# The last norm of a two-layer encoder: 1/rms by ScalarE's root and a Newton step on VectorE, and the last quarter's squares and sum in one VectorE instruction

## The chip, the cores and the metric

The kernel runs on one core of one Trainium2 chip. A core has five engines that each work through a queue of their own, in order: TensorE (PE in the profile; PEld is its loading of weights), VectorE (DVE), ScalarE (ACT), GpSimd (POOL) and SyncE (SP, which here only starts transfers). They wait for one another by semaphores. The metric is the time of one execution on the device, in microseconds; lower is better. The profile is that of one execution; it has a span (first to last instruction) that is a little shorter than the time.

## The reference

Two layers over 512 frames of 1024 channels: a half-step SwiGLU feed-forward block, a mixing block of two head groups, cross-attention into 256 memory tokens, and a second half-step feed-forward block. Behind the last layer stands a norm. All is float32.

```python
def rmsnorm(x, g):
    xf = x.astype(jnp.float32)
    y = xf * lax.rsqrt(jnp.mean(xf * xf, axis=-1, keepdims=True) + EPS)
    return (y * g.astype(jnp.float32)).astype(x.dtype)

def swiglu(h, w1, w3, w2):
    return (jax.nn.silu(h @ w1) * (h @ w3)) @ w2

def reference(...):
    for l in range(DEPTH):
        x = x + 0.5 * swiglu(rmsnorm(x, ffn1_norm[l]), ffn1_w1[l], ffn1_w3[l], ffn1_w2[l])
        ...
        x = x + 0.5 * swiglu(rmsnorm(x, ffn2_norm[l]), ffn2_w1[l], ffn2_w3[l], ffn2_w2[l])
    return rmsnorm(x, final_norm)
```

The change is in the last line: the norm of the result, frame by frame, and what stands around it at the end of the program.

## The kernel before

Through nearly all of the program the activations lie transposed, channels on the 128 partitions and the 512 frames in the columns. Weights come in by transfers from SyncE (some are added to others on the way by transfers that GpSimd starts, line 134); ScalarE and VectorE split each weight into a rounded high part and the rest (lines 76 and 77), and a product is three matmuls (`mm3`, lines 84 to 86).

The last block is `finish`. There the second product of the last feed-forward block is computed with frames on the partitions, so that a frame's norm is a sum along a row. There are four blocks of 128 frames; `y[i]` holds block i, 128 x 1024. `turn(i)` first brings the residual into `y[i]` (transposes on TensorE, copies on ScalarE, line 1127). Blocks 0 and 1 are accumulated together, weight by weight, in four PSUM tiles of 512 columns. Then TensorE makes block 2 in two halves, then the first half of block 3 (`k` in the code), then its second half in two quarters of 256 columns, and ends.

For each piece `add` adds half of the PSUM tile to `y` on VectorE (line 1132), and ScalarE squares the result with a sum along the row into a column of `ss` (line 1134, fss in the profile; an ACTIVATE and the reading of the accumulator). `sums` adds two such columns and makes v = sum/1024 + 1e-6 on VectorE (lines 1138 and 1139, fv). `scale` then takes v to the power -1/2 on GpSimd (line 1146, fcol), multiplies both halves of `y` by that column and by the gain on VectorE (lines 1150 and 1152), and sends them out, the first half from ScalarE's queue (line 1151) and the second from SyncE's (line 1153).

Block 3 is the one that ends the program. Its first half is multiplied by the gain ahead of time (line 1180), so that ScalarE can scale it by the column alone (`ahead`, line 1148) while VectorE does the second half. Its v is made from the first three quarters ahead of time, and the last quarter's sum is added by line 1188.

What order these instructions have on each engine is decided by the framework's scheduler when the program is built, from the order of the code and a model of times; the engines then keep to it. At the program's end, line 1297, SyncE waits for all outputs to land, each engine drains (it waits until what it has started is done) and reports to GpSimd by a semaphore, and GpSimd lets all of them go; this happens twice.

Of the kernel before, what the change touches and what calls it, by code (L numbers as in the profile page):

```python
# [7 lines left out]
F32 = mybir.dt.float32  # L8
F32R = mybir.dt.float32r
I32 = mybir.dt.int32  # L10
AF = mybir.ActivationFunctionType
ALU = mybir.AluOpType
AX = mybir.AxisListType

P = 128
D = 1024
# [30 lines left out]
def trunk_kernel(ctx: ExitStack, tc: tile.TileContext, ap: dict, out: bass.AP):  # L47
    nc = tc.nc
    pe, act, dve, pool = nc.tensor, nc.scalar, nc.vector, nc.gpsimd
# [3 lines left out]
    tp = ctx.enter_context(tc.tile_pool(name="tp", bufs=2))  # L53
    sm = ctx.enter_context(tc.tile_pool(name="sm", bufs=3))
# [3 lines left out]
    def acc_tile():  # L58
        return pacc.tile([P, 512], F32, tag="acc", name="acc")

    def ps_tile():
        return pp.tile([P, 512], F32, tag="ps", name="ps")
# [5 lines left out]
    def s_tile(shape, dt, name):  # L68
        return sp.tile(shape, dt, tag="s", name=name)
# [12 lines left out]
    def mm3(o, a, b, start, stop, more=False):  # L82

        pe.matmul(o, a[0], b[0], start=start, stop=False, skip_group_check=more)  # L84
        pe.matmul(o, a[0], b[1], start=False, stop=False, skip_group_check=more)  # L85
        pe.matmul(o, a[1], b[0], start=False, stop=stop, skip_group_check=more)  # L86
# [205 lines left out]
    nhalf = const.tile([P, 4], F32, name="nhalf")  # L292
# [822 lines left out]
    def finish(a):  # L1115
        n = len(a)
        gain = s_tile([P, D], F32, "gain")
        nc.scalar.dma_start(gain, ap["final_norm"].broadcast_to([P, D]))
        y = [s_tile([P, D], F32, "y") for _ in range(NT)]
        ss = sm.tile([P, NT, 3], F32, tag="fss", name="fss", bufs=1)  # L1120

        def turn(i):
            for hf in range(2):
                ps = ps_tile()
                for c in range(4):
                    pe.transpose(ps[:, c * P:(c + 1) * P], xT[hf * 4 + c][:, i * P:(i + 1) * P], ident)
                act.copy(y[i][:, hf * 512:(hf + 1) * 512], ps)

        def add(i, at, ps, lo, hi):

            yi = y[i][:, lo:hi]
            dve.scalar_tensor_tensor(yi, ps, 0.5, yi, op0=ALU.mult, op1=ALU.add)
            sq = tp.tile([P, 512], F32, tag="sq", name="fsq", bufs=4)
            act.activation(sq[:, :hi - lo], yi, AF.Square, accum_out=ss[:, i, at:at + 1])

        def sums(i):
            v = sm.tile([P, 1], F32, tag="fv", name="fv", bufs=4)
            dve.tensor_tensor(v, ss[:, i, 0:1], ss[:, i, 1:2], op=ALU.add)
            dve.tensor_scalar(v, v, 1.0 / D, EPS, op0=ALU.mult, op1=ALU.add)
            return v  # L1140

        def scale(i, v, ahead=False):

            y0, y1, sl = y[i][:, :512], y[i][:, 512:], slice(i * P, (i + 1) * P)
            col = sm.tile([P, 1], F32, tag="fcol", name="fcol", bufs=4)
            pool.tensor_tensor(col, v, nhalf[:, 0:1], op=ALU.pow)
            if ahead:
                act.activation(y0, y0, AF.Copy, scale=col)
            else:
                dve.scalar_tensor_tensor(y0, y0, col, gain[:, :512], op0=ALU.mult, op1=ALU.mult)  # L1150
            nc.scalar.dma_start(out[0, sl, :512], y0)
            dve.scalar_tensor_tensor(y1, y1, col, gain[:, 512:], op0=ALU.mult, op1=ALU.mult)
            nc.sync.dma_start(out[0, sl, 512:], y1)

        w = {}

        def products(ps, i, js, lo, hi):
            sl = slice(i * P, (i + 1) * P)
            for j in js:
                mm3(ps, (a[j][0][:, sl], a[j][1][:, sl]), (w[j][0][:, 0, lo:hi], w[j][1][:, 0, lo:hi]), start=j == 0, stop=j == n - 1)  # L1160


        accs = {(i, hf): acc_tile() for i in range(2) for hf in range(2)}
        for j in range(n):
            w[j] = wts.next()
            for i, hf in accs:
                products(accs[i, hf], i, [j], hf * 512, (hf + 1) * 512)
                if j == n - 1:
                    add(i, hf, accs[i, hf], hf * 512, (hf + 1) * 512)
            if j < NT:  # L1170
                turn(j)
        i, k, js = 2, 3, range(n)
        accs = {(x, hf): ps_tile() for x in (i, k) for hf in range(2)}
        for hf in range(2):
            products(accs[i, hf], i, js, hf * 512, (hf + 1) * 512)
            add(i, hf, accs[i, hf], hf * 512, (hf + 1) * 512)
            scale(hf, sums(hf))
        products(accs[k, 0], k, js, 0, 512)
        add(k, 0, accs[k, 0], 0, 512)
        dve.tensor_tensor(y[k][:, :512], y[k][:, :512], gain[:, :512], op=ALU.mult)  # L1180
        scale(i, sums(i))
        for q in range(2):
            lo, ps = 512 + 256 * q, (accs[k, 1] if q else acc_tile())[:, :256]
            products(ps, k, js, lo, lo + 256)
            add(k, 1 + q, ps, lo, lo + 256)
            if q == 0:
                v = sums(k)
        dve.tensor_scalar(v, ss[:, k, 2:3], 1.0 / D, v, op0=ALU.mult, op1=ALU.add)
        scale(k, v, ahead=True)


    idle = ps_tile()
# [38 lines left out]
    for l in range(L):  # L1231
        nxt = Norm("mix_norm", l)
        if l == 0:
            ffn(norm, PLAIN[0], nxt.add, start=begin, between=early())
        else:
            ffn(norm, PLAIN[2], nxt.add)
        norm, nxt = nxt, Norm("xa_norm", l, row=False)
        mn = []
        mem = memory(l, mn)
        mix(l, norm, mem, nxt.add)  # L1240
        for _ in mem:
            pass
        norm, nxt = nxt, Norm("ffn2_norm", l)
        xattn(l, norm, mn, nxt.add)
        norm = nxt
        if l + 1 < L:
            nxt = Norm("ffn1_norm", l + 1)
            ffn(norm, PLAIN[1], nxt.add)
            norm = nxt
        else:  # L1250
            finish(ffn(norm, PLAIN[3], None))
# [49 lines left out]
```

## Time and profile before

| | us |
|---|---|
| time, median of 3 runs (lowest, highest) | 2092.37 (2092.34, 2093.55) |
| time of the profiled execution | 2092.47 |
| its span | 2090.7 |
| busy in it: PE, DVE, ACT, POOL | 2077.4, 1408.4, 918.0, 230.3 |
| TensorE's mean granted clock | 0.999 of full speed |

In the profile's rows a line stands for the instructions of one line of the kernel on one engine: the tile it writes, an arrow, what it reads, partitions x columns, and how many there are. In a timeline the first number is the start and the second the duration, both in us; in brackets stands how long the engine had been idle, and behind an arrow what ended that. An engine's name with a q is its queue: drains, semaphores and the starting of transfers, which aren't counted as busy.

### The profile page before, as it was taken

What the parts mean: (1) busy time and instruction counts of PE and PEld (TensorE: products, weight loads), DVE (VectorE), ACT (ScalarE), POOL (GpSimd) and SP (SyncE); (2) the same over time, 40 slices, a digit from 0 to 9 for tenths busy, and PEclk for the clock granted to TensorE, in tenths of its full rate; (3) what the DMA queues carried; (4) which work ended last, traced back from release to release, by engine and by line L of the source; (5) the groups of instructions that cost most, each with busy time, mean ns of one, the idle gap of its engine ahead of it and who ended that gap; (6) DMA issues with size and microseconds to landing.
All of it is one profiled execution on the core that took longest, in us unless ns stands there. A gap on an engine that the chain in (4) does not pass through costs nothing.

```text
span 2090.7 us, 29622 instructions
## 1 busy us (share of the span) xinstructions
PE 2077.4 (99%) x11538; PEld 1798.0 (86%) x11538; DVE 1408.4 (67%) x2126; ACT 918.0 (44%) x1461; POOL 230.3 (11%) x240
## 2 busy tenths in 40 slices
PE   9999999999999999999999999999999999999998
PEld 8889898888888888989888898988788888889897
DVE  7758576687655575766776685758766547668574
ACT  6425345434444343434544353445345434435253
POOL 1100000331000020000020000003410001100000
PEclk9999999999999999999999999999999999999999
DMA  5364554233432246636415646532343331574541
GB/s 188 115 186 121 147 157 156 67 101 108 140 121 87 61 131 186 156 118 176 131 61 158 190 111 184 156 104 71 102 117 130 101 116 41 152 203 129 140 143 71
DMA packets 109533, 268.35 MB, mean 128 GB/s; under 512 B 11536, under 2 KB 14608, under 8 KB 109392
## 3 DMA queue, kind: packets, MB, share of 16 engines
q1 hardware_dynamic: 93952, 224.49, 32.8%
q0 software_dynamic: 13104, 39.07, 10.6%
q10 hardware_dynamic: 2336, 2.89, 0.5%
q8 instruction: 91, 1.49, 0.3%
q14 instruction: 50, 0.41, 0.1%
HBM read 256.70 MB, written 2.10 MB: 124 GB/s over the span
## 4 chain that ended last, share of the span: by engine, by line
PE 97%; DVE 2%; issue 1%; POOL 0%; ACT 0%; POOLq 0%; DVEq 0%; ACTq 0%
PE ps L86 19%; PE ps L84 19%; PE ps L85 18%; PE acc L554 8%; PE acc L84 8%; PE acc L85 8%; PE acc L86 8%; PE acc L555 4%; PE ps L1030 1%; PE ps L1031 1%; PE ps L796 1%; DVE wlo L77 0%; PE ps L979 0%; PE ps L1096 0%; PE acc L346 0%
## 5 line engine op out<-in xcount | busy, mean ns | idle before, releaser
L77 DVE TENSOR_TENSOR wlo<-raw,whi 128x1024 fp32r<-128x1024 f32 (+1 forms) x334 | 394.5, 1202 | 72.0 <-ACT whi L76 63.7
L76 ACT CAST whi<-raw 128x1024 fp32r<-128x1024 f32 (+1 forms) x334 | 330.2, 1017 | 118.1 <-DMA raw<-in_ffn_w_dram 47.6
L85 PE MATMUL ps<-h,whi 128*128 128x512 f32 x848 | 330.0, 389 | 0.0
L84 PE MATMUL ps<-h,whi 128*128 128x512 f32 x848 | 329.9, 391 | 0.0
L86 PE MATMUL ps<-h,wlo 128*128 128x512 f32 x848 | 329.7, 390 | 0.0
L554 PE MATMUL acc<-bhl,whi 128*128 128x512 f32 x744 | 266.3, 398 | 0.0
L86 PE MATMUL ps<-bhl,wlo 128*128 128x256 f32 x744 | 210.8, 284 | 0.2
L85 PE MATMUL ps<-bhl,whi 128*128 128x256 f32 x744 | 209.9, 283 | 0.0
L84 PE MATMUL ps<-bhl,whi 128*128 128x256 f32 x744 | 209.8, 283 | 0.0
L555 PE MATMUL acc<-bhl,wlo 128*128 128x256 f32 x744 | 204.8, 281 | 0.0
L76 ACT CAST whi<-wsum 128x1024 fp32r<-128x1024 f32 x124 | 130.2, 1050 | 151.3 <-DVE wsum L165 83.9
L86 PEld LDWEIGHTS ps<-h,wlo 128*128 128x128 f32 x848 | 159.2, 188 | 33.5
L85 PEld LDWEIGHTS ps<-h,whi 128*128 128x128 f32 x848 | 159.2, 188 | 33.0
L84 PEld LDWEIGHTS ps<-h,whi 128*128 128x128 f32 x848 | 159.1, 188 | 32.9
L77 DVE TENSOR_TENSOR wlo<-wsum,whi 128x1024 fp32r<-128x1024 f32 x124 | 151.5, 1222 | 49.6 <-ACT whi L76 47.3
L554 PEld LDWEIGHTS acc<-bhl,whi 128*128 128x128 f32 x744 | 137.7, 189 | 24.0
L84 PEld LDWEIGHTS ps<-bhl,whi 128*128 128x128 f32 x744 | 141.5, 190 | 4.1
L86 PEld LDWEIGHTS ps<-bhl,wlo 128*128 128x128 f32 x744 | 141.4, 190 | 2.5 <-DVE wlo L77 1.6
L555 PEld LDWEIGHTS acc<-bhl,wlo 128*128 128x128 f32 x744 | 141.0, 190 | 2.8
L85 PEld LDWEIGHTS ps<-bhl,whi 128*128 128x128 f32 x744 | 141.6, 190 | 1.9
L134 POOL DMA_DIRECT2D wsum<-in_ffn_w_dram x62 | 53.8, 867 | 765.0 <-DMA wsum<-in_ffn_w_dram 369.6
L84 PE MATMUL acc<-ahl,whi 128*128 128x512 f32 x328 | 128.0, 390 | 0.0
(272 smaller groups left out, 4127.5 us busy)
## 6 DMA issues: line engine op xcount, KB each, us to landing
raw<-in_ffn_w_dram SPq DMA_DIRECT2D x198, 512.0 KB
wsum<-in_ffn_w_dram SPq DMA_DIRECT2D x124, 256.0 KB
wsum<-in_ffn_w_dram POOLq DMA_DIRECT2D x62, 512.0 KB, 6.7
raw<-in_w_in_dram SPq DMA_DIRECT2D x32, 512.0 KB
raw<-in_ffn_w_dram SPq DMA_DIRECT2D x62, 256.0 KB
raw<-in_w_out_dram SPq DMA_DIRECT2D x16, 512.0 KB
raw<-in_xa_wk_dram SPq DMA_DIRECT2D x16, 512.0 KB
raw<-in_xa_wq_dram SPq DMA_DIRECT2D x16, 512.0 KB
```

Source lines behind the costliest of these rows:

```text
L76: act.copy(hi, src)
L77: dve.tensor_tensor(lo, src, hi.bitcast(F32), op=ALU.subtract)
L84: pe.matmul(o, a[0], b[0], start=start, stop=False, skip_group_check=more)
L85: pe.matmul(o, a[0], b[1], start=False, stop=False, skip_group_check=more)
L86: pe.matmul(o, a[1], b[0], start=False, stop=stop, skip_group_check=more)
L134: nc.gpsimd.dma_start(s1, c2, accum_op=ALU.add)
L554: pe.matmul(ps.rearrange("p (c t) -> p c t", t=HT), w[0], t, start=start and k == 0, stop=False, skip_group_check=True)
L555: pe.matmul(ps[:, :HT], w[1], t[:, 0], start=False, stop=k == 3, skip_group_check=True)
L796: pe.matmul(ps[hh * 64:hh * 64 + 64, o:o + 64], keys[g][:, c:c + 64], b, start=True, stop=True)
L1030: pe.matmul(ps.rearrange("p (c m) -> p c m", m=M), whl[0][:, k], mn[k], start=k == 0, stop=False, skip_group_check=True)
L1031: pe.matmul(ps[:, :M], whl[1][:, k], mn[k][:, 0], start=False, stop=k == NK - 1, skip_group_check=True)
```

## The change

A new function `inverse` makes the column without GpSimd: s = the root of v on ScalarE, r = 1/s on VectorE, e = v r r, t = 1.5 - e/2, and r t is the result, a Newton step, since the root comes from a table. It is four VectorE instructions on 128x1 columns, each of which needs the one before. `scale` uses it for blocks 0, 1 and 2.

Block 3 has a function of its own, `last`. The squares of the last quarter and their sum are one VectorE instruction, which also adds v (it starts its sum with it); its place in the listing is two rows, the operation and the reading of its accumulator. The last quarter's add stands by itself, without ScalarE's square. The gain is multiplied in ahead of the column for all 1024 columns, the third quarter's before the sum of the first three, the last quarter's behind the reduction. What remains behind the column is one scaling per half: ScalarE's copy with a scale, as before, and a VectorE multiplication by a column with no gain.

```diff
-        def scale(i, v, ahead=False):
+        def inverse(v):
+            root = sm.tile([P, 4], F32, tag="froot", name="froot", bufs=4)
+            s, r, e, t = (root[:, c:c + 1] for c in range(4))
+            act.activation(s, v, AF.Sqrt)
+            dve.reciprocal(r, s)
+            dve.tensor_scalar(e, v, r, r, op0=ALU.mult, op1=ALU.mult)
+            dve.tensor_scalar(t, e, -0.5, 1.5, op0=ALU.mult, op1=ALU.add)
+            dve.tensor_tensor(s, r, t, op=ALU.mult)
+            return s
+
+        def scale(i, v):
 
             y0, y1, sl = y[i][:, :512], y[i][:, 512:], slice(i * P, (i + 1) * P)
-            col = sm.tile([P, 1], F32, tag="fcol", name="fcol", bufs=4)
-            pool.tensor_tensor(col, v, nhalf[:, 0:1], op=ALU.pow)
-            if ahead:
-                act.activation(y0, y0, AF.Copy, scale=col)
-            else:
-                dve.scalar_tensor_tensor(y0, y0, col, gain[:, :512], op0=ALU.mult, op1=ALU.mult)
+            col = inverse(v)
+            dve.scalar_tensor_tensor(y0, y0, col, gain[:, :512], op0=ALU.mult, op1=ALU.mult)
             nc.scalar.dma_start(out[0, sl, :512], y0)
             dve.scalar_tensor_tensor(y1, y1, col, gain[:, 512:], op0=ALU.mult, op1=ALU.mult)
             nc.sync.dma_start(out[0, sl, 512:], y1)
+
+        def last(i, v):
+            y0, y1, sl = y[i][:, :512], y[i][:, 512:], slice(i * P, (i + 1) * P)
+            q, sq = y1[:, 256:], tp.tile([P, 512], F32, tag="sq", name="fsq", bufs=4)
+            full = sm.tile([P, 1], F32, tag="fv", name="fv", bufs=4)
+            dve.tensor_tensor_reduce(sq[:, :256], q, q, 1.0 / D, v, ALU.mult, ALU.add, full)
+            dve.tensor_tensor(q, q, gain[:, 768:], op=ALU.mult)
+            col = inverse(full)
+            act.activation(y0, y0, AF.Copy, scale=col)
+            nc.scalar.dma_start(out[0, sl, :512], y0)
+            dve.tensor_scalar(y1, y1, col, None, op0=ALU.mult)
+            nc.sync.dma_start(out[0, sl, 512:], y1)
...
             products(ps, k, js, lo, lo + 256)
-            add(k, 1 + q, ps, lo, lo + 256)
             if q == 0:
+                add(k, 1, ps, lo, lo + 256)
+                dve.tensor_tensor(y[k][:, 512:768], y[k][:, 512:768], gain[:, 512:768], op=ALU.mult)
                 v = sums(k)
-        dve.tensor_scalar(v, ss[:, k, 2:3], 1.0 / D, v, op0=ALU.mult, op1=ALU.add)
-        scale(k, v, ahead=True)
+            else:
+                dve.scalar_tensor_tensor(y[k][:, 768:], ps, 0.5, y[k][:, 768:], op0=ALU.mult, op1=ALU.add)
+        last(k, v)
```

Lines count anew from here: in the changed kernel the root is line 1146, the four VectorE steps are 1147 to 1150, `scale`'s products 1157 and 1159, the reduction 1167, the last quarter's gain 1168, the last two scalings 1170 and 1172, and the program ends at line 1319.

The scheduler's order shows what moves. On VectorE, behind the four adds of blocks 0 and 1 (froot is the tile of the root's four columns), the order before was this:

```order
L1132 SCALAR_TENSOR_TENSOR y<-acc,y 128x512 [waits PE_49,Activation_49] x2
L1138 TENSOR_TENSOR fv<-fss 128x1 [waits Activation_49]
L1139 TENSOR_SCALAR fv<-fv 128x1 [waits DVE_49]
L1138 TENSOR_TENSOR fv<-fss 128x1 [waits Activation_49]
L1150 SCALAR_TENSOR_TENSOR y<-y,fcol,gain 128x512 [waits DMAHW7_49,Pool_49]
L1152 SCALAR_TENSOR_TENSOR y<-y,fcol,gain 128x512
L1139 TENSOR_SCALAR fv<-fv 128x1 [waits DVE_49]
L1132 SCALAR_TENSOR_TENSOR y<-ps,y 128x512 [waits PE_49]
```

In the changed kernel the same place reads:

```order
L1138 TENSOR_TENSOR fv<-fss 128x1 [waits Activation_49]
L1147 RECIPROCAL froot<-froot 128x1 [waits Activation_49]
L1139 TENSOR_SCALAR fv<-fv 128x1 [waits DVE_49]
L1148 TENSOR_SCALAR froot<-fv,froot 128x1 [waits DVE_49]
L1147 RECIPROCAL froot<-froot 128x1 [waits Activation_49]
L1149 TENSOR_SCALAR froot<-froot 128x1 [waits DVE_49]
L1148 TENSOR_SCALAR froot<-fv,froot 128x1 [waits DVE_49]
L1150 TENSOR_TENSOR froot<-froot 128x1 [waits DVE_49]
L1149 TENSOR_SCALAR froot<-froot 128x1 [waits DVE_49]
L1157 SCALAR_TENSOR_TENSOR y<-y,froot,gain 128x512 [waits DMAHW7_49,DVE_49]
L1159 SCALAR_TENSOR_TENSOR y<-y,froot,gain 128x512
L1150 TENSOR_TENSOR froot<-froot 128x1 [waits DVE_49]
```

The Newton steps of blocks 0 and 1 stand interleaved ahead of block 0's output, and the second block's sum (the second L1139) stands behind the first reciprocal, which waits for ScalarE. On ScalarE one table load has come in, at the first root, behind the four squares of blocks 0 and 1; a piece of the difference:

```order
 L1134 ACTIVATE fsq,fss<-y 128x512 x4
-L1151 DMA out_dram<-y 128x512
+L1146 ACT_TABLE_LOAD
+L1146 ACTIVATE froot<-fv 128x1 x2
+L1158 DMA out_dram<-y 128x512
```

There is no other load behind it up to the end. At VectorE's end, from the add of block 3's third quarter on, the changed kernel has these rows (the two called ISA are the reduction and the reading of its accumulator):

```order
L1132 SCALAR_TENSOR_TENSOR y<-acc,y 128x256 [waits PE_49]
L1200 TENSOR_TENSOR y<-y,gain 128x512 [waits Activation_49]
L1207 TENSOR_TENSOR y<-y,gain 128x256 [waits Activation_49]
L1138 TENSOR_TENSOR fv<-fss 128x1
L1139 TENSOR_SCALAR fv<-fv 128x1 [waits DVE_49]
L1210 SCALAR_TENSOR_TENSOR y<-ps,y 128x256 [waits PE_49]
L1167 ISA fsq,fv<-y,fv 128x256 [waits DVE_49]
L1167 ISA fv 128x1
L1168 TENSOR_TENSOR y<-y,gain 128x256 [waits DVE_49]
L1147 RECIPROCAL froot<-froot 128x1 [waits Activation_49]
L1148 TENSOR_SCALAR froot<-fv,froot 128x1 [waits DVE_49]
L1149 TENSOR_SCALAR froot<-froot 128x1 [waits DVE_49]
```

Before, one instruction (L1188) stood between the last add and the last output there, and the first half's gain stood ahead of the third quarter's add, not behind it. At GpSimd's end this piece of the difference shows what is its last instruction:

```order
 L134 DMA wsum<-in_ffn_w_dram 128x1024 x14
-L1146 TENSOR_TENSOR fcol<-fv,nhalf 128x1 x4
-L1297 UNCONDITIONAL_BRANCH
-L1297 ISA
+L1319 UNCONDITIONAL_BRANCH
+L1319 ISA
```

The four powers are gone, and the weight transfers are followed by the program's end.

## The prediction

> **What bounds the kernel now.** I read the first part of the page, then the timeline of the last 15 us, then the rows of the program's last line, and last the prices of single operations.
>
> ```profile
> span 2090.7 us, 29622 instructions
> PE 2077.4 (99%) x11538; PEld 1798.0 (86%) x11538; DVE 1408.4 (67%) x2126; ACT 918.0 (44%) x1461; POOL 230.3 (11%) x240
> ```
>
> TensorE is busy for 99% of the span, and the change touches none of its instructions. What it can move is what stands behind the last matmul, or something that stops TensorE before it. The timeline shows the tail (start, duration, engine, line, operation):
>
> ```profile
> 2080.62 0.28 PE L86 MATMUL ps<-whi,ahl 128*128 128x256 f32 x1
> 2080.93 0.42 DVE L1132 SCALAR_TENSOR_TENSOR y<-ps,y 128x256 f32<-128x256 f32 x1 [0.75 <-PE ps L86]
> 2081.45 0.42 ACT L1134 ACTIVATE fsq<-y 128x256 f32<-128x256 f32 x1 [1.65 <-DVE y L1132]
> 2081.78 0.19 ACT L1134 ACTIVATION_READ_ACCUMULATOR fsq<-y 128x1 f32 x1
> 2081.99 0.21 DVE L1188 TENSOR_SCALAR fv<-fss,fv 128x1 f32<-128x1 f32 x1 [0.64 <-ACT fsq L1134]
> 2082.29 0.54 POOL L1146 TENSOR_TENSOR fcol<-fv,nhalf 128x1 f32<-128x1 f32 x1 [7.23 <-DVE fv L1188]
> 2082.86 0.72 ACT L1148 ACTIVATE y<-y,fcol 128x512 f32<-128x512 f32 x1 [0.90 <-POOL fcol L1146]
> 2082.87 0.75 DVE L1152 SCALAR_TENSOR_TENSOR y<-y,fcol,gain 128x512 f32<-128x512 f32 x1 [0.66 <-POOL fcol L1146]
> 2083.62 0.37 ACTq L1151 DMA_DIRECT2D out_dram<-y  x1
> 2083.64 0.33 SPq L1153 DMA_DIRECT2D out_dram<-y  x1
> ```
>
> So the last add ends at 2081.35, the root is there at 2082.83, and the last two output transfers are issued by 2083.99. The span ends 6.7 us later. The rows of L1297, the line at which the program ends, say what fills that (count, min/median/max ns, first and last start); the second fence is the same view over a narrow window, the third the waits of SyncE's queue, the fourth the chain of waits, the last the program's first line:
>
> ```profile
> L1297 POOLq EVENT_SEMAPHORE  x4: 17/17/17, 2090.0 to 2090.6; - x4
> L1297 POOLq DRAIN  x3: 46/97/7656, 2082.3 to 2090.4; - x3
> ```
> ```profile
> L1297 SPq DRAIN  x2: 7/7/7, 2086.9 to 2087.0; - x2
> ```
> ```profile
> SPq L1297 <- DMA out_dram<-y: 2.4, 1, 2.4
> ```
> ```profile
> 2082.25 0.59 POOLq L1297
> ```
> ```profile
> L1291 POOLq DRAIN  x1: 184/184/184, 0.3 to 0.3; - x1
> ```
>
> SyncE waits 2.4 us for the output to land, works through its semaphores, and its second drain is done at 2087.0. GpSimd's queue came to its drain at 2082.25, behind the last power, and that drain takes 7.656 us, to 2089.91. Only then do GpSimd's semaphores follow (2090.0), and 0.79 us after the drain the span ends. So **the end of the program waits 2.9 us for GpSimd's drain alone** (2087.0 to 2089.91), which is 7.08 us beyond the end of GpSimd's last instruction (2082.83). A drain is not slow in itself: the one at the start took 0.184 us behind four small fills, the shortest at the end 0.046.
>
> **The change, part by part.** *GpSimd loses its four powers.* Its last instruction is then the weight transfer:
>
> ```profile
> 2003.21 0.85 POOL L134 DMA_DIRECT2D wsum<-in_ffn_w_dram  x1 [9.29 <-PE ps L86]
> ```
> ```profile
> wsum<-in_ffn_w_dram POOLq DMA_DIRECT2D x62, 512.0 KB, 6.7
> ```
>
> The queue reaches its drain at 2004.1, 83 us before SyncE is done. No row shows how long the drain then takes. Ends: 0.18 us (the start's) to 14.4 us (the 6.7 that such a transfer takes to land, by the page's list of issues, and then 7.66); both are far inside 83 us. So if the drain belongs to GpSimd's own queue, the whole 2.9 us goes, and SyncE's drain is late next. I take that: between 2087.0 and 2089.91 nothing else in the trace ends.
>
> *The new chain behind the last add.* These rows price it:
>
> ```profile
> 2078.17 0.69 DVE L1180 TENSOR_TENSOR y<-y,gain 128x512 f32<-128x512 f32 x1 [0.85 <-ACT fsq L1134]
> 2078.78 0.42 DVE L1132 SCALAR_TENSOR_TENSOR y<-acc,y 128x256 f32<-128x256 f32 x1
> 2079.84 0.16 DVE L1138 TENSOR_TENSOR fv<-fss 128x1 f32<-128x1 f32 x1 [0.64 <-ACT fsq L1134]
> 2080.03 0.15 DVE L1139 TENSOR_SCALAR fv<-fv 128x1 f32<-128x1 f32 x1
> L77 DVE TENSOR_TENSOR kT<-kf,kT 128x256 fp32r<-128x256 f32 x16 | 6.7, 418 | 0.2
> 2077.41 0.63 ACT L1134 ACTIVATE fsq<-y 128x512 f32<-128x512 f32 x1 [3.36 <-DVE y L1132]
> L1070 DVE RECIPROCAL su<-su x8: 170/175/178, 611.6 to 1657.6; 128x4 f32<-128x4 f32 x8
> L1072 DVE TENSOR_SCALAR p<-p,su x32: 346/349/355, 611.8 to 1658.6; 128x256 f32<-128x256 f32 x32
> ```
>
> A VectorE instruction that needs the one before it starts 0.03 after its end (2080.00 to 2080.03); one that doesn't starts 0.08 before it (2078.86 and 2078.78). From the add's end at 2081.35:
>
> - squares and sum in one instruction: 0.03, then 0.42 as the two-input 128x256 of the kT row: 2081.80. No row has a VectorE accumulator's reading; nearest is a 128x1 operation, 0.16, less the overlap of 0.08; from 0 to 0.19 (a wait in between). I take 0.08: 2081.88.
> - the last quarter times the gain stands ahead of the reciprocal: 0.03 + 0.42: 2082.33.
> - beside it the root on ScalarE. 0.63 for 512 columns and 0.42 for 256 leave 0.21 for none, and another engine's result reached ScalarE in 0.03 (2082.83 to 2082.86): 2082.12. It is hidden by the multiply, up to 0.34 dear.
> - reciprocal: starts 0.08 before the multiply's end, 0.17: 2082.42.
> - square of it times v: L1188 with one column as scalar took 0.21, L1139 with none 0.15, so two make 0.27 (0.21 if the second is free): 2082.72. Half-and-three-halves 0.03 + 0.15: 2082.90. The last product 0.03 + 0.16: 2083.09.
> - ScalarE's copy 0.03 later, 0.72 as before: 2083.84, where it was 2083.58. **The tail gets 0.26 us longer** on ScalarE's side.
> - VectorE's half: 0.349 for 256 less 0.21 makes 0.14 for each 256 columns, so 0.49 where 0.75 stood: 2083.12 to 2083.61, as before (2083.62). Its transfer keeps its time.
>
> What goes is 1.48 us (2081.35 to 2082.83, square, sum, power), what comes is 1.74.
>
> Weighed against a rule: L1152 reads two fp32 tiles of SBUF and a column, and 0.75 is what L1180's 0.69 and 0.06 for a column make; no slower pace is seen, though nothing there accumulates. The Trainium skill, "Vector Engine (DVE) Microarchitecture Reference", section "7. Points that are easy to get wrong", says that an accumulating two-source operation on two SBUF sources that aren't bf16 runs at half pace. No run here shows that form; by the rule the sum grows as in the second case below.
>
> *Ahead of the tail.* VectorE works in order, and its first reciprocal now waits for a root behind a table load:
>
> ```profile
> 37.99 1.28 ACT L689 ACT_TABLE_LOAD   x1
> 39.28 0.63 ACT L689 ACTIVATE t<-t 128x512 f32<-128x512 f32 x1
> 2066.12 0.19 ACT L1134 ACTIVATION_READ_ACCUMULATOR fsq<-y 128x1 f32 x1
> 2068.47 0.69 DVE L1132 SCALAR_TENSOR_TENSOR y<-ps,y 128x512 f32<-128x512 f32 x1 [0.53 <-PE ps L86]
> 2072.55 0.69 DVE L1132 SCALAR_TENSOR_TENSOR y<-ps,y 128x512 f32<-128x512 f32 x1 [2.07 <-PE ps L86]
> 2076.63 0.69 DVE L1132 SCALAR_TENSOR_TENSOR y<-ps,y 128x512 f32<-128x512 f32 x1
> 2079.62 0.18 ACT L1134 ACTIVATION_READ_ACCUMULATOR fsq<-y 128x1 f32 x1
> ```
>
> A load takes 1.28 and the next instruction follows at once. From 2066.31: load to 2067.6, root to 2067.8, then two interleaved Newton steps, eight small instructions at 0.19: the first output starts about 2069.4. Queued behind it are the add of 2068.47 (about 2070.9 now) and the second block's output; the add of 2072.55 comes at 2072.9, 0.3 late. The third block's root adds 0.3 more, so the add of 2076.63 starts near 2077.2. There lateness ends: the add of 2078.78 waits for TensorE, not for VectorE. Behind it stand two multiplies by the gain, of which the second waits for ScalarE's sum at 2079.80, then L1138 and L1139: done at 2080.55, 0.38 us before the last add can start. TensorE itself waits for none of these: its last products go to PSUM tiles that nothing has to free, except one that the first adds freed before the sums of 2066.31. So all this costs nothing, with 0.38 us to spare; beyond that each us late is a us at the end.
>
> **Sum.** Against the profiled execution: SyncE's drain at 2087.0 + 0.26, then 0.79: the span ends at 2088.06 in place of 2090.7, 2.64 less. That execution took 2092.47 in all, so 2089.83. It lay 0.10 above the median of the runs (2092.37, from 2092.34 to 2093.55), so **2089.8**.
>
> **The rivals.**
>
> *Half pace of the reduction* (0.27 more for 256 columns: 0.69 in place of 0.42): 2090.1. Against it speaks L1152's full pace; for it, that no row accumulates.
>
> *The drain stays at the end.* If what GpSimd's drain waits for is not its own last instruction but the end of everything (output landed and a fixed time behind), its place in the queue doesn't matter. It decides from the moment at which the drain ends: 2.91 us behind SyncE's. Then nothing is won and the longer tail shows: 2092.47 + 0.26 = 2092.7, slower than before (2092.5 if its end is fixed, 2093.0 with half pace). For it: 7.08 us with nothing running on GpSimd has no cause in the trace. Against it: SyncE's and ScalarE's drains there are short, and the output's landing is 2.9 us away from its end. The Trainium skill, "VectorE: DVE Perf Modes", section "The DRAIN you can't avoid", has the drains at a kernel's ends as some 12 ns, the same on all engines; 7656 ns here is no such thing, so by that page GpSimd's would be waiting for something, which is this case.
>
> *Tables reloaded at every change between root and square or copy.* Two loads in the tail, one hidden by nothing: 2089.8 + 2 x 1.28 = 2092.4. The new order has a single load, so this would be the change not doing what it says.
>
> **How the numbers follow.** Forecast 0.62, half pace 0.15, drain stays 0.17, reloads 0.03, the rest 0.03 (0.01 a gain over 4.2 us, 0.02 a TensorE stop that costs as much). The first two, with the tail's bounds (0.08 and 0.06 less; 0.11 more for the accumulator's reading and 0.08 for a reciprocal that can't overlap) and 0.4 us for runs, lie between 2089.3 and 2090.7 and hold 0.75, too little; so the range reaches over the drain's case: 2089.3 to 2092.9. A measurement here can tell 0.2%, that is 4.2 us, from no change; neither a gain of 2.6 us nor a loss of 0.5 passes it. Faster 0.01, same 0.97, slower 0.02.
>
> **What would show it.** Right: GpSimd's long drain starts near 2004, its first closing semaphore stands right behind SyncE's drain near 2087.3, the span is 2088.1; one table load near 2066.3; the last add still at 2080.93; ScalarE's last copy at 2083.1. Wrong: a drain of GpSimd that still ends 2.9 us behind SyncE's; a last add later than 2080.93 (the slack was too small); a reduction of 0.69; a copy that starts other than 0.26 later.

## The result, and the profile after

| | before | changed |
|---|---|---|
| median of 22 runs (lowest, highest), us | 2092.51 (2091.6, 2094.39) | 2089.27 (2088.45, 2090.37) |
| profiled execution: time, span, us | 2092.47, 2090.7 | 2089.08, 2087.2 |

The ratio is 0.9984, with a 95% interval of 0.9978 to 0.9990: 3.2 us less, with 2.1 to 4.6 as bounds. The interval leaves out a ratio of 1, so the measurement tells more than the 0.2% (4.2 us) that the prediction gave it. The forecast was 2089.8 in a range of 2089.3 to 2092.9; the measured 2089.27 lies 0.03 us below the range.

The rows of line 1319, where the changed kernel ends (count, min/median/max ns, first and last start):

```profile
L1319 POOLq EVENT_SEMAPHORE  x4: 17/17/17, 2086.5 to 2087.1; - x4
L1319 POOLq DRAIN  x3: 46/98/10083, 2002.8 to 2086.9; - x3
L1319 SPq DRAIN  x3: 7/7/7, 2086.4 to 2086.7; - x3
```

GpSimd's long drain now starts at 2002.8 and lasts 10.08 us, so it is over at 2012.9, and GpSimd's first closing semaphore (2086.5) stands right behind SyncE's drain (2086.4). Before, 3.0 us lay between (2087.0 to 2090.0). The timeline of the tail:

```profile
2080.51 0.42 DVE L1210 SCALAR_TENSOR_TENSOR y<-ps,y 128x256 f32<-128x256 f32 x1 [0.41 <-PE ps L86]
2080.97 0.48 DVE L1167 CUSTOM_DVE_ANT_0 fsq<-y,fv 128x256 f32<-128x256 f32 x1
2081.38 0.08 DVE L1167 DVE_READ_ACCUMULATOR2_ANT fv<- 128x1 f32 x1
2081.50 0.20 ACT L1146 ACTIVATE froot<-fv 128x1 f32<-128x1 f32 x1 [2.11 <-DVE fv L1167]
2081.50 0.43 DVE L1168 TENSOR_TENSOR y<-y,gain 128x256 f32<-128x256 f32 x1
2081.84 0.16 DVE L1147 RECIPROCAL froot<-froot 128x1 f32<-128x1 f32 x1
2082.04 0.27 DVE L1148 TENSOR_SCALAR froot<-fv,froot 128x1 f32<-128x1 f32 x1
2082.34 0.15 DVE L1149 TENSOR_SCALAR froot<-froot 128x1 f32<-128x1 f32 x1
2082.53 0.16 DVE L1150 TENSOR_TENSOR froot<-froot 128x1 f32<-128x1 f32 x1
2082.72 0.72 ACT L1170 ACTIVATE y<-y,froot 128x512 f32<-128x512 f32 x1 [1.02 <-DVE froot L1150]
2082.72 0.49 DVE L1172 TENSOR_SCALAR y<-y,froot 128x512 f32<-128x512 f32 x1
2083.24 0.33 SPq L1173 DMA_DIRECT2D out_dram<-y  x1
2083.48 0.34 ACTq L1171 DMA_DIRECT2D out_dram<-y  x1
```

The two rows of line 1167 are the reduction and its accumulator's reading. The last add ends at 2080.94, the column is there 1.75 us later, and ScalarE issues the last transfer 2.54 us behind the add, where it was 2.26: the longer chain is really there. But it doesn't show in the end. The windows of half a microsecond show why (start and end, length, the five engines' busy times, which are nothing here, then the granted TensorE clock, the share of the 16 DMA engines and GB/s); first before, then changed:

```profile
2084.00:2084.50 0.50, 0.00 (x0) 0.00 (x0) 0.00 (x0) 0.00 (x0) 0.00 (x0) 1.00 0.07 25
2084.50:2085.00 0.50, 0.00 (x0) 0.00 (x0) 0.00 (x0) 0.00 (x0) 0.00 (x0) 0.91 0.99 377
2085.00:2085.50 0.50, 0.00 (x0) 0.00 (x0) 0.00 (x0) 0.00 (x0) 0.00 (x0) 0.50 1.02 389
2085.50:2086.00 0.50, 0.00 (x0) 0.00 (x0) 0.00 (x0) 0.00 (x0) 0.00 (x0) 0.50 0.71 258
```
```profile
2084.00:2084.50 0.50, 0.00 (x0) 0.00 (x0) 0.00 (x0) 0.00 (x0) 0.00 (x0) 1.00 0.86 315
2084.50:2085.00 0.50, 0.00 (x0) 0.00 (x0) 0.00 (x0) 0.00 (x0) 0.00 (x0) 1.00 1.02 381
2085.00:2085.50 0.50, 0.00 (x0) 0.00 (x0) 0.00 (x0) 0.00 (x0) 0.00 (x0) 0.77 0.92 348
```

In both kernels the two halves of block 3, 512 KB together, keep all 16 DMA engines busy for some 1.4 us. Before, they left together and shared the engines; now SyncE's half leaves 0.24 us ahead of ScalarE's, which finds the engines taken: its first packet comes 1.28 us behind its issue, where ScalarE's transfers of blocks 0 to 2 took 0.85.

### The profile page after: what moved, and what is told of

Its sections match the earlier page's. It is cut to its first block, busy times and chain, and to the rows that moved or that the text cites. A ratio compares the mean times of both kernels' runs of the same rounds, so it can differ in the third digit from the quotient of the medians.

```text
span 2087.2 us, 29640 instructions
## 1 busy us (share of the span) xinstructions
PE 2077.6 (100%) x11538; PEld 1798.1 (86%) x11538; DVE 1411.7 (68%) x2145; ACT 919.7 (44%) x1464; POOL 228.1 (11%) x236
## 3 DMA queue, kind: packets, MB, share of 16 engines
q8 instruction: 91, 1.49, 0.3%
## 4 chain that ended last, share of the span: by engine, by line
PE 97%; DVE 2%; POOL 0%; issue 0%; ACT 0%; DVEq 0%; POOLq 0%
PE ps L86 19%; PE ps L84 19%; PE ps L85 19%; PE acc L554 8%; PE acc L84 8%; PE acc L85 8%; PE acc L86 8%; PE acc L555 4%; PE ps L1030 1%; PE ps L1031 1%; PE ps L796 1%; DVE wlo L77 0%; PE ps L979 0%; PE ps L1096 0%; PE acc L346 0%; PE ps L1219 0%
```

## The experiments

In what follows "behind the add" is counted from the end of block 3's last add, since TensorE's end differed between executions: that add ended anywhere from 2080.7 to 2082.0 in the profiled executions of this study's big kernels, and TensorE's instructions are the same in all of them. Times are compared for the first three runs and the last version, which ran eleven times each; the others ran once and are read by the rows of their profile. The short diffs are against the changed kernel.

**Is it GpSimd's drain, and its last instruction that counts?** Three runs. In the first GpSimd's power makes block 3's column again:

```diff
-            col = inverse(full)
+            col = sm.tile([P, 1], F32, tag="fcol", name="fcol", bufs=4)
+            pool.tensor_tensor(col, full, nhalf[:, 0:1], op=ALU.pow)
```

> The changed kernel, but block 3's column comes from GpSimd's power again (the only one left in the last block, and GpSimd's last instruction). My theory: the program's end waits for GpSimd's drain whenever GpSimd has an instruction late in the tail. The power then ends about 1.15 us behind the last add, its drain about 7.1 us later, and the span 0.79 us behind that: 9.0 us behind the last add, where it is 6.28 in the changed kernel and 9.34 before. Time: 2.7 us above the changed kernel, 0.3 below the kernel before, so near 2092.2. Rival (the gain comes from VectorE's and ScalarE's shorter work and the drain only ends with the program): the outputs are issued 0.6 us earlier than in the changed kernel, so the time is that of the changed kernel or up to 0.6 below it, 2088.7 to 2089.3.

In the second it makes the columns of blocks 0 to 2, and block 3 keeps the root and the Newton step (the same edit in `scale`, with v in place of full):

> The changed kernel, but blocks 0 to 2 take their column from GpSimd's power, block 3 from the root and the Newton step. My theory: only the last use of GpSimd counts. Its last power ends some 5.5 us before the last add starts, its drain about 7.1 us later, before the outputs have landed: the time of the changed kernel, 2089.3, and a span that ends 6.3 us behind the last add. Rival (any use of GpSimd in the last block costs, since its drain follows the program's end or grows with the number of instructions): 2092 or more, as before.

In the third everything stays as changed, and GpSimd copies a column that nothing reads:

```diff
+            idle_col = sm.tile([P, 1], F32, tag="fcol", name="fcol", bufs=4)
+            pool.tensor_copy(idle_col, full)
             col = inverse(full)
```

> The changed kernel with one more instruction: GpSimd copies block 3's sum into a column that nothing reads, so nothing waits for it but the program's end. Theory a (a drain behind any GpSimd instruction is long): GpSimd's drain ends some 7 us behind the copy, the span 8.5 to 9 us behind the last add, the time 2.3 to 2.7 us above the changed kernel, near 2091.8. Theory b (the power alone leaves the long drain): a drain of 0.1 to 0.3 us, span and time as in the changed kernel, 2089.3.

Measured, on one chip, against 2092.72 before: 2092.35 for the first (ratio 0.9999, 0.9990 to 1.0008), 2089.34 for the second (0.9985, 0.9976 to 0.9994), 2092.05 for the third (0.9997, 0.9989 to 1.0006). GpSimd's timeline and the drains of the first:

```profile
2081.66 0.81 POOL L1170 TENSOR_TENSOR fcol<-fv,nhalf 128x1 f32<-128x1 f32 x1 [77.90 <-DVE fv L1167]
L1320 POOLq DRAIN  x3: 46/98/7926, 2081.6 to 2090.1; - x3
```

of the second (its last power):

```profile
2074.44 0.55 POOL L1157 TENSOR_TENSOR fcol<-fv,nhalf 128x1 f32<-128x1 f32 x1 [5.96 <-DVE fv L1139]
L1320 POOLq DRAIN  x3: 46/98/7661, 2074.4 to 2087.3; - x3
```

and of the third:

```profile
2081.81 0.44 POOL L1170 COPY fcol<-fv 128x1 f32<-128x1 f32 x1 [77.64 <-DVE fv L1167]
L1321 POOLq DRAIN  x3: 46/98/7537, 2081.8 to 2089.8; - x3
```

The drain ends 7.08 us behind the end of GpSimd's last instruction in all of them as before the change (to the ns of the trace: 7077, 7077, 7077 and 7078 ns for before and the three), whether that is a power or a copy and whether anything waits for it. In the second it is over at 2082.1, ahead of the output, and the whole gain is there with three powers left in the last block: the span ends 6.28 us behind the add, as in the changed kernel. In the third a copy that no one reads takes the gain away (8.90 us). So the gain is GpSimd's place in the tail; the root, the Newton step and the reduction bring none of it by themselves. In the first run the output is issued at 1.97 and 2.21 us behind the add and SyncE's drain is done at 5.19, 0.3 us ahead of the changed kernel's 5.51, and the drain of GpSimd hides that. Its span ends at 9.29 and not at the 9.0 expected, since its power took 0.81 us where 0.54 was taken from before.

**What makes the drain long?** A fill in place of the copy, in the changed kernel (`pool.memset(full, 0.0)` behind the last use of it):

> The changed kernel with one more instruction: GpSimd fills block 3's sum with zero once nothing needs it any more. So far the drain ended 7.08 us behind GpSimd's last power or copy, whatever it was. Theory a (a drain is long behind anything GpSimd computes late in this program): 7.1 us behind the fill again, the span some 9 us behind the last add. Theory b (only operations that read something, as power and copy do, leave a long drain; the program's first drain stood behind four fills and took 0.18 us): a drain of at most 0.3 us behind the fill and a span of 6.28 us behind the last add.

```profile
2082.96 0.10 POOL L1172 MEMSET fv<- 128x1 f32 x1 [79.68 <-DVE froot L1148]
L1320 POOLq DRAIN  x3: 46/98/7186, 2083.0 to 2090.7; - x3
```

Theory a: 7.186 us from 2082.95, again 7.08 behind the fill's end. Power, copy and fill make no difference to it. Then small kernels, which only move x, multiply it by one and let GpSimd copy a column at the end; they leave out the whole encoder.

> Not the program: a small kernel that loads x by four transfers from SyncE, multiplies it 40 times by one on VectorE, lets GpSimd copy one column as its last instruction, and stores x. GpSimd starts no transfer at all. Theory a (the 7.08 us are the drain's own price behind an instruction of GpSimd): drain ends 7.1 us behind the copy. Theory b (the 7.08 us come from transfers that GpSimd started earlier in the program, whose rings the drain has to go through): a drain of 0.1 to 0.4 us.

> The small kernel with the same work, but the four loads are started by GpSimd, some 20 us ahead of its copy. Both theories say 7.1 us behind the copy if the drain of the kernel without such transfers was long too; if that one was short, theory b says 7.1 here (if the length doesn't go by the number of transfers) or less than that (if it does; the big kernel started 119).

> The small kernel with 36 more transfers started by GpSimd ahead of its loads, 256 KB each and read by nothing: 40 transfers, 11.5 MB. The drain ended 0.07 us behind GpSimd's copy without such transfers, 0.41 with 4 (576 packets, 2.1 MB), 7.08 in the big kernel with 119 (13104 packets, 39.07 MB). A line through the last two gives for this one 2.5 us if the drain goes by the number of transfers, 3.2 by packets (5760), 2.1 by bytes.

> The same with the 36 transfers 8 KB each: 40 transfers, 5760 packets, 2.4 MB. By number 2.5 us, by packets 3.2, by bytes 0.5. All three fall if the drain stays near 0.4: then its length goes by something else in the big kernel.

> The small kernel with 119 transfers started by GpSimd, as many as the big kernel starts: 115 of 8 KB each and the four loads. Behind the copy the drain took 0.07 us with no such transfer, 0.41 with 4, and 3.35 with 40, whether these were of 8 or of 256 KB, so it goes by the number, 0.08 us for each. If it goes on so: 9.8 us here. If it is bounded, or goes by how many transfers were started since some point, as the big kernel's 7.08 suggests: 7.08 (a bound that counts transfers) or another value under 9.8.

Each fence has the drains of one of them, in this order: no transfer from GpSimd, 4, 40 (36 of them 256 KB), 40 (36 of them 8 KB), 119.

```profile
L40 POOLq DRAIN  x3: 34/76/273, 28.7 to 33.9; - x3
```
```profile
L40 POOLq DRAIN  x3: 34/95/612, 29.4 to 34.7; - x3
```
```profile
L43 POOLq DRAIN  x3: 34/95/3552, 55.5 to 60.9; - x3
```
```profile
L43 POOLq DRAIN  x3: 34/95/3554, 48.6 to 54.0; - x3
```
```profile
L43 POOLq DRAIN  x3: 40/95/1354, 91.3 to 96.7; - x3
```

In these kernels the long drain comes from the transfers that GpSimd started earlier, although the last of them had landed some 21 us before: it ends 0.07 us behind the copy without any, 0.41 with 4, 3.35 with 40. Bytes don't matter (11.5 and 2.4 MB give the same), nor do packets (3456 and 1728 in the records; the 5760 of the expectation was a miscount), and from 0 over 4 to 40 it is 0.08 us for each transfer. But with 119 it is 1.15 and not the 9.8 of that line, and in the big kernel, with 119 as well, 7.08. So the number of transfers alone isn't the rule beyond 40. Perhaps it is the number since some point in the program; GpSimd issued the 119 one behind the other with a single break, of 0.47 us, ahead of the 114th, but the six from there on would give some 0.6 us at 0.08 each, not 1.15. That was not settled. Nor did a run take the 119 transfers out of the big kernel: that its 7.08 us come from them is concluded from the small ones.

**Why did the longer chain not show?** The gain of block 3's second half is put back behind the column, so that its scaling takes longer and both halves leave together:

```diff
-            dve.tensor_tensor(q, q, gain[:, 768:], op=ALU.mult)
             col = inverse(full)
...
-            dve.tensor_scalar(y1, y1, col, None, op0=ALU.mult)
+            dve.scalar_tensor_tensor(y1, y1, col, gain[:, 512:], op0=ALU.mult, op1=ALU.mult)
...
-                dve.tensor_tensor(y[k][:, 512:768], y[k][:, 512:768], gain[:, 512:768], op=ALU.mult)
```

> The changed kernel, but the second half of block 3 is multiplied by the gain together with the column, as before, so the multiply ahead of the reciprocal goes and VectorE's last instruction takes 0.75 in place of 0.49 us. Behind the last add's end I expect ScalarE's transfer issued at 2.43 (2.54 in the changed kernel) and SyncE's at 2.46 (2.30). My theory for the 0.25 us that the prediction had too much (the two halves share the DMA engines, so the end of both is set by the first issue and the bytes): first issue 2.43 in place of 2.30, so the span ends 0.13 later behind the last add, 6.41 in place of 6.28. Rival (the later issue sets the end): 0.08 earlier, 6.20.

In the next ScalarE scales 640 columns and VectorE 384 (`y0, y1 = y[i][:, :640], y[i][:, 640:]` in `last`, and the transfers with them):

> The changed kernel, but ScalarE scales 640 of block 3's columns and VectorE 384, in place of 512 each. Issues behind the last add: ScalarE's 2.65 in place of 2.54, SyncE's 2.23 in place of 2.30. If the first issue and the bytes set the end (my theory, borne out when both issues fell together): span 0.07 us earlier, 6.21, or 6.28 where the DMA engines run dry in between. If the later issue sets it: 0.11 later or, with its larger transfer, up to 0.3 later, 6.39 to 6.6.

And a version that uses what these showed, with three VectorE instructions for the inverse and the second half in two transfers. The inverse of the first two lines is a copy made for block 3; what is left out of the diff is the factor -1/2 in block 3's gains, which the shorter step needs, and the last quarter's multiply ahead of the column, which goes:

```diff
-            dve.tensor_scalar(t, e, -0.5, 1.5, op0=ALU.mult, op1=ALU.add)
-            dve.tensor_tensor(s, r, t, op=ALU.mult)
+            dve.tensor_scalar(t, e, -3.0, r, op0=ALU.add, op1=ALU.mult)
...
-            dve.tensor_scalar(y1, y1, col, None, op0=ALU.mult)
-            nc.sync.dma_start(out[0, sl, 512:], y1)
+            dve.tensor_scalar(p, p, col, None, op0=ALU.mult)
+            nc.sync.dma_start(out[0, sl, 512:768], p)
+            dve.scalar_tensor_tensor(q, q, col, gain[:, 768:], op0=ALU.mult, op1=ALU.mult)
+            nc.sync.dma_start(out[0, sl, 768:], q)
```

> A version to beat the changed kernel: in block 3 the Newton step is three VectorE instructions (the last makes r(e - 3), which is -2 times the result; the gains of block 3 carry the factor -1/2), the last quarter's gain goes in with the column, so no multiply stands ahead of the reciprocal, and the second half leaves in two transfers, the third quarter's first. Behind the last add's end: column at 1.52 (1.75 in the changed kernel), first issue 1.93 (2.30), the last two 2.30 to 2.33 (2.54). If the first issue and the bytes set the end, as the two runs on it showed: the outputs land 0.3 to 0.4 us earlier, span 5.9 to 6.0 us behind the last add in place of 6.28. If the last issue sets it: 0.2 earlier, 6.07. By time the same as the changed kernel, 2088.9 to 2089.0 against 2089.3, which the rounds can't tell apart.

Measured, in us behind the add, from the trace's records of these three and of the two main kernels (p and q are the third and the last quarter):

| kernel | SyncE's issue | ScalarE's issue | first packet | last packet's end | SyncE's drain | span's end |
|---|---|---|---|---|---|---|
| before | 2.29 | 2.26 | 3.11 | 4.64 | 5.64 | 9.34 |
| changed | 2.30 | 2.54 | 3.13 | 4.65 | 5.51 | 6.28 |
| gain behind | 2.47 | 2.44 | 3.29 | 4.81 | 5.80 | 6.56 |
| 640 and 384 | 2.27 | 2.64 | 3.10 | 4.62 | 5.48 | 6.25 |
| three transfers | 1.97 (p), 2.40 (q) | 2.31 | 2.80 | 4.42 | 5.29 | 6.06 |

In the first four rows the 512 KB take 1.52 us from first packet to last, however the issues lie to one another (up to 0.37 us apart). With 640 columns ScalarE's issue is 0.10 later and the end 0.03 earlier, as the first issue is: the rival (0.11 to 0.3 later) falls. The 0.07 expected did not come because SyncE's issue moved less than was reckoned (to 2.27, not 2.23). With the gain behind, ScalarE's issue is 0.10 earlier and the last packet 0.16 later. The span's end is 0.29 later, more than the 0.13 expected: with both halves landing together SyncE has one wait more to work through behind the last packet (0.06), and the first of these waits ends 0.43 us behind that packet in place of 0.37. This second part (0.13 together) I read off the rows and did not test by itself.

What the rows don't tell apart is the first issue and SyncE's issue. In all five the first packet comes 0.83 us behind SyncE's first issue, and where ScalarE's is the earlier one it is so by 0.03 us only.

The version with three transfers ends 0.22 us earlier behind the add than the changed kernel, short of the 0.3 to 0.4 that first issue and bytes gave: its 512 KB took 1.62. Its windows:

```profile
2083.50:2084.00 0.50, 0.00 (x0) 0.00 (x0) 0.00 (x0) 0.00 (x0) 0.00 (x0) 1.00 1.01 338
2084.00:2084.50 0.50, 0.00 (x0) 0.00 (x0) 0.00 (x0) 0.00 (x0) 0.00 (x0) 0.67 1.00 381
2084.50:2085.00 0.50, 0.00 (x0) 0.00 (x0) 0.00 (x0) 0.00 (x0) 0.00 (x0) 0.50 0.91 311
```

The engines don't run dry. By the trace's packets, the two quarters go in packets of 1 KB, where the halves go in 2 KB, and all packets together take 1.49 us of each DMA engine, where they take 1.40 in the other four rows. The first issue 0.33 earlier and 0.09 more of packets' time give 6.03. By the expectations as they stand, 5.9 to 6.0 and 6.07, the measured 6.06 misses the first and meets the second; but the second had the last issue at 2.33, and with the measured 2.40 it would give 6.13. So this run lies 0.03 us from first issue and packets' time and 0.07 from the last issue, which is too little to decide it. By time it is 2089.46 (ratio to before 0.9985, 0.9976 to 0.9994), the same as the changed kernel.

## Why the prediction was wrong, point by point

**The main step held.** "The end of the program waits 2.9 us for GpSimd's drain alone": the drain behind the last transfer took 10.08 us, within the 0.18 to 14.4 that the prediction allowed and far inside the 83 us that it had. With the drain gone from the tail SyncE's is late next, as written, and the runs with a late power, an early power and a late copy show that it is GpSimd's last instruction that decides. The rival by which the drain stays at the end falls with them. The sentence of the Trainium skill on which that rival leaned ("VectorE: DVE Perf Modes", "The DRAIN you can't avoid": some 12 ns on all engines) doesn't hold for GpSimd here: 67 to 7078 ns behind a computing instruction.

**The step that failed is a term of the sum**: "The tail gets 0.26 us longer on ScalarE's side", carried on as "SyncE's drain at 2087.0 + 0.26". ScalarE's issue did come 0.28 us later behind the add, but what ends last there is the landing, and the landing did not move: 4.64 us behind the add before and 4.65 after. The prediction itself had VectorE's half keep its time, and did not ask what the two transfers share: with SyncE's half first, ScalarE's waits for DMA engines that are busy anyway.

As for size: the tail lost 3.06 us in place of 2.64 (9.34 to 6.28). The 0.42 are those 0.26; 0.08 from the last packet to SyncE's wait and 0.06 for a semaphore wait less behind it; and 0.03 in the closing round of semaphores (0.01 by which the landing came later goes off). The run with the gain behind, whose halves land together as before, has nearly all of the 0.08 and the 0.06 back. Why the 0.08 is less with the halves apart stays open: with three transfers it is back too (0.44 us from the last packet to the wait), though one transfer alone is still out there. Nothing in the range allowed for the term to vanish: its low end took 0.14 for the chain and 0.4 for the runs. A bound of nothing for a delay ahead of a shared transfer would have put the low end at 2089.2 (2089.83 - 0.26 - 0.4). That the measured median lies 0.03 below the range and not just inside it is chance; its runs reach from 2088.45 to 2090.37.

A slip of the sum: it names 0.10 by which the profiled execution lay above the median of three runs, and then doesn't take it off, which would have made 2089.73. The median of 22 runs of the kernel before is 2092.51, 0.04 above that execution, so there was no 0.10 to take off.

The medians lie 3.24 apart, the two spans 3.48. In the profiled executions TensorE's end was 0.42 earlier in the changed kernel, which no instruction explains and which is within the scatter of that add between the profiled kernels (2080.7 to 2082.0); the runs can't tell 3.06 from 3.24.

**The chain's prices.** Predicted 1.74 us from the add's end to the column's, measured 1.75. The reduction took 0.48 where 0.42 stood in the sum (its scalar column costs 0.06, as in L1188's row); its accumulator's reading ended 0.01 behind it, where 0.08 stood. These two misses cancel, so that the chain came right to 0.01 is partly luck. The reduction runs at the pace of the other two-input operations, so the rival of half pace (0.69) falls. With it falls the use made here of the rule of the Trainium skill, "Vector Engine (DVE) Microarchitecture Reference", section "7. Points that are easy to get wrong". That section of the Trainium skill does not say from which pace it halves. A scaling of one input here took 0.13 us for 256 more columns (0.35 and 0.49) where two inputs took 0.27, so the reduction may already be at half of a faster pace, and the rows don't refute the rule itself. The root took 0.20 for 0.21, the product with two columns 0.27 as taken.

**Ahead of the tail.** One table load came, and nothing was late at the end. ScalarE and VectorE around it, in the changed kernel:

```profile
2065.91 1.28 ACT L1146 ACT_TABLE_LOAD   x1
2067.20 0.20 ACT L1146 ACTIVATE froot<-fv 128x1 f32<-128x1 f32 x1
2068.52 0.75 DVE L1157 SCALAR_TENSOR_TENSOR y<-y,froot,gain 128x512 f32<-128x512 f32 x1
2072.12 0.69 DVE L1132 SCALAR_TENSOR_TENSOR y<-ps,y 128x512 f32<-128x512 f32 x1 [0.20 <-PE ps L86]
2079.95 0.15 DVE L1139 TENSOR_SCALAR fv<-fv 128x1 f32<-128x1 f32 x1
```

The first output starts 0.5 us sooner than "about 2069.4", after the 0.42 by which TensorE was ahead: interleaved, the small instructions started as little as 0.08 apart. The add that was to be 0.3 late waited for TensorE instead. L1139 was done at 2080.10, 0.41 before the last add; 0.38 was predicted. The rival of reloaded tables falls.

## What to carry to other kernels

Look at what ends the program, not only at the last output: the drain of each engine's queue is a row of its own, and where GpSimd has started transfers, see how long its drain is (here 0.41 to 7.08 us behind the last computing instruction) and have its last instruction that much ahead of the end, be it a power, a copy or a fill. Where two transfers leave side by side and keep the DMA engines busy, as here with issues up to 0.37 us apart, the first issue and the time of the packets set the end, so time on the later one is hidden and time on the first one is not. A delay ahead of something shared is to be bounded from nothing up, and that end kept in the range.

## What the runs showed of the hardware

In the small kernels GpSimd's drain grew by 0.08 us for each transfer that GpSimd had started, up to 40, whether of 8 or of 256 KB, some 21 us after the last had landed; with 119 it ended 1.15 us behind the copy in a small kernel and 7.08 in the big one. Directly behind a transfer as GpSimd's last instruction it lasted 10.1 us. Two transfers of 256 KB from SyncE and ScalarE took 1.52 us from the first packet to the last with issues 0.03 to 0.24 us apart. The late power took 0.81 us, where it took 0.54 to 0.57 before. It came after 78 us without an instruction on GpSimd, and beside a VectorE multiply (L1168, 0.56 to 0.99 us behind the add; the power began at 0.62). The first power of the kernel before came after 61.8 us without one, beside no VectorE multiply, and took 0.57, so the multiply is the likelier cause; that was not tested.
